# A two-layer attention and recurrence step on one core: engine queues ordered by the scheduler's finer timing model, first loads pinned in program order

## The chip, the cores and the metric

The kernel runs on 1 core of one Trainium2 chip. The metric is the device time of one launch in microseconds. The kernel before took 906.66 us (median of 3 runs, 905.13 to 910.31). In what follows PE is TensorE, ACT is ScalarE, DVE is VectorE, POOL is GpSimd and SP is SyncE; SP issues the loads that matter here.

## The reference

One inference step of a trunk of two layers over 128 context tokens and 512 latent tokens of width 1024. Each layer modulates its input by a shift and scale from SiLU(cond), mixes the tokens, gates the branch by a SiLU path, projects it out, and ends in a residual and a layer norm. Layer 0 mixes by grouped attention (16 heads, 4 key heads, rotary positions), layer 1 by HGRN2, a gated linear recurrence over 8 heads with one scan forward and one backward. Cut to what matters:

```python
for i in range(DEPTH):                       # 2 layers
    hp = xp * (1.0 + sc_p) + sh_p            # context;  hs likewise for latent tokens
    if i == 0:
        out_p, kp, vp = _attn_context(hp, ...)
        out_s = _attn_latent(hs, cache_k, cache_v, ...)
    else:
        out_p, sp_fw, sp_bw = _rec_mix(hp, zeros, zeros, ...)
        out_s, _, _ = _rec_mix(hs, state_fw, state_bw, ...)
    xp = _layer_norm(alpha * xp + g_p * out_p, ...)

def _rec_mix(h, s0_fw, s0_bw, w_in, lb, norm_gain, w_out):
    q, f_fw, f_bw, i_in, g = split(h @ w_in)             # five blocks of 1024 columns
    forget = lb + (1 - lb) * sigmoid(f); inp = (1 - lb) * sigmoid(-f)   # per direction
    # per head and direction: S_t = forget_t * S_{t-1} + inp_t v_t^T,  o_t = q_t S_t
    o = _rms_norm(o_fw + o_bw, norm_gain)
    return (o * silu(g)) @ w_out, s_fw, s_bw
```

The outputs are both token streams, the context's new keys and values, and its new states.

## The kernel before, in words

**Numbers.** Products are done in fp32r with operands split into a high and a low part: hi·hi, hi·lo and lo·hi are three matmuls. A weight piece of 128 x 1024 is loaded as fp32 by SP (`pump`, L198 to L211) into a ring of raw buffers; `split_piece` (L217) casts the high part on ACT (L221) and subtracts it on DVE or POOL (L222). `pump` is called ahead of and behind every split and issues loads in the order of a list, as far as the rings have room.

**Order of the work.** The program is written as generators that are woven by hand: `weave` puts projection steps beside the attention, and `Lane` steps a recurrence generator beside a projection generator by the estimated time of each step (the gaps D_LEV, D_KT and so on). The framework's scheduler then sets the order of each engine's queue from dependencies and a timing model, and puts in the semaphore waits. Each engine executes its queue in order; where an instruction must wait, those behind it in the same queue wait too.

**Stages, as the trace has them.** 0 to 72 us: x is transposed on PE (L443), the modulation computed (L264), x modulated (L450), keys and values projected (L469 to L471). 72 to 375: attention, scores L740 and L741, probabilities L835 and L838, transposes L850, product with the values L767; the query, gate and modulation projections (L334 to L336, L325 to L327, L264) lie beside it. 375 to 459: output projection (L1021 to L1023) and layer norm. 459 to 812: the recurrence, a head's projection overlapping the recurrence of the head before. 812 to 902.7: the last head's recurrence, then output projection, norm and stores.

**A head's projection** (`proj_gen`, L1098). Value and gate columns: 120 matmuls `vgps` (L1133 to L1135). Then three groups i = 0, 1, 2 (q and the two gates) of 48 matmuls `rps` (L1143 to L1145), called R below. Each group needs its weight piece split: cast L221 into `rhi`, a ring of two buffers, so that the cast of a later piece waits until the R that read that buffer are done; then subtraction L222 into `rlo`. Each group ends in an eviction: sigmoid `s` (L1165), for i = 1, 2 also a second sigmoid `s_…` (L1175) and a scaling (L1176) on ACT, and products on DVE.

**A head's recurrence** (`gla_gen`, L1240), called by the lane. It has seven levels of doubling block width. A level is 20 or 40 small matmuls `lv` (L1273 for levels 0 to 4, L1279 for 5 and 6), then a product on DVE that updates the keys in `A` (L1282), a copy `kc` of them on ACT (L1251, levels 0 to 3), a product on DVE that updates the queries (L1287), and a merge of the result (L1263). The next level's matmuls need both products and `kc`. Level 4 also has the diagonal `dg` (L1297). After level 6: transposes `kp` (L1313), their copy `kt` on ACT (L1315), state products `sp` (L1319), a chain of six state updates on DVE (L1322, L1325), the output products `op` (L1336 to L1339), squares and root (L1344, L192), normalization on DVE (L1348, L1350), transposes `oT` (L1355). The last head has no projection beside it; `tail_gen` gives it gate matmuls (`gateps`, L294) and the first output matmuls (`outp`, L1021 to L1023).

Of the kernel before, what the change touches and what calls it, by code (L numbers as in the profile page):

```python
# [18 lines left out]
P = 128  # L19
D = 1024  # L20
KT = D // P
TS = 4
# [115 lines left out]
def hybrid_step(ctx: ExitStack, tc: tile.TileContext, a: dict, o: dict):  # L138
    nc = tc.nc
# [54 lines left out]

    ahead = deque()
    order = deque()

    def pump():  # L198
        while order:
            start = order[0] in FIRST  # L200
            if len(ahead) >= (RAW_START if start else RAW_AHEAD):
                break
            src = order.popleft()
            if src[0] == "x":
                c = slice(src[1] * CW, (src[1] + 1) * CW)
                nc.sync.dma_start(xt[:, :TS, c], a["xs"][:, c].rearrange("(t p) d -> p t d", p=P))
                nc.sync.dma_start(xt[:, TS, c], a["xp"][:, c])
                continue
            raw = (raw0 if start else rawp).tile([P, 1024], F32, tag="raw", name="raw")
            nc.sync.dma_start(raw, piece(src))  # L210
            ahead.append((src, raw))  # L211

    def piece(src):
        name, c, i = src
        return a[name][c][:, i * 1024:(i + 1) * 1024]

    def split_piece(hi, lo, src, lo_eng=None):  # L217
        pump()
        got, raw = ahead.popleft()
        assert got == src, (got, src)  # L220
        nc.scalar.copy(hi, raw)  # L221
        (lo_eng or nc.gpsimd).tensor_tensor(lo, raw, hi.bitcast(F32), ALU.subtract)  # L222
        pump()
# [28 lines left out]
    def take(src):  # L252
        pump()
        got, raw = ahead.popleft()
        assert got == src, (got, src)
        return raw
# [123 lines left out]
    def lpool(name, bufs):  # L380
        return left.enter_context(pool(name, bufs))
# [8 lines left out]
    xt = gsp.tile([P, TT, D], F32, tag="gs", name="xt")  # L390
# [1042 lines left out]
    xp = lpool("xp", 3)  # L1433
# [102 lines left out]
```

## Time and profile before

| what | value |
|---|---|
| median of 3 runs | 906.66 us (905.13 to 910.31) |
| the profiled execution | 904.83 us |
| its span | 902.7 us |
| mean granted PE clock | 0.987 |
| PE busy | 853.8 us (95%) |
| DVE, ACT, POOL busy | 560.8, 374.2, 217.9 us |
| PE busy in 518 to 800 | 281.54 of 282.00 us |

The span runs from the first to the last instruction that the profile shows; the profiled execution's own time is 2.1 us longer. Busy time counts an instruction from its start to its modelled end, and matmuls overlap, so that the difference between two starts is the time a matmul takes up. The granted clock is given as a share of full speed. In a row of the timeline the brackets give the idle time of the engine ahead of the instruction, and the instruction that ended it.

### The profile page before, as it was taken

To read this page: it belongs to the slowest core of one execution; us is meant where nothing else is said; L and a number is where in the kernel's file an instruction comes from. 1 tells how busy PE (TensorE), PEld (TensorE's weight loads), DVE (VectorE), ACT (ScalarE), POOL (GpSimd) and SP (SyncE) were. 2 spreads that over 40 slices of the span, in tenths; PEclk is the share of its full clock that TensorE was granted. 3 is DMA by queue.
4 is the path that set the end of the run, shared out by engine and by line. 5 is a ranking of instruction groups with operands and counts; after the bars stand their busy time and mean duration, and the time that the engine had idled before them with its cause. 6 is when DMAs were issued, how large, how long until landed. Compare 5 with 4: busy or idle time off the path is not lost.

```text
span 902.7 us, 19256 instructions
## 1 busy us (share of the span) xinstructions
PE 853.8 (95%) x8116; PEld 741.6 (82%) x8116; DVE 560.8 (62%) x990; ACT 374.2 (41%) x735; POOL 217.9 (24%) x251
## 2 busy tenths in 40 slices
PE   5999999999999799899999999999999999998995
PEld 3779978777777686567889999999999999996774
DVE  3466565566576565377644667585858575859495
ACT  2142565456345544532243444444444444345200
POOL 2013033233123315340000133224241404120110
PEclk9999999999999799999999999999999999998998
DMA  9932021212030224563131322323132332223121
GB/s 318 330 106 82 24 79 41 94 49 94 24 117 25 94 71 147 185 224 144 55 95 48 95 84 78 99 75 96 53 110 71 88 90 89 84 70 137 54 94 70
DMA packets 32678, 89.86 MB, mean 100 GB/s; under 512 B 4400, under 2 KB 11568, under 8 KB 32592
## 3 DMA queue, kind: packets, MB, share of 16 engines
q1 hardware_dynamic: 21984, 71.57, 23.4%
q0 software_dynamic: 3264, 9.51, 3.9%
q10 hardware_dynamic: 7344, 7.55, 2.6%
q8 instruction: 64, 1.05, 0.5%
q14 instruction: 22, 0.18, 0.1%
HBM read 79.44 MB, written 9.18 MB: 98 GB/s over the span
## 4 chain that ended last, share of the span: by engine, by line
PE 81%; DVE 8%; ACT 3%; DMA 3%; POOL 3%; issue 2%; SPq 0%; DVEq 0%; ACTq 0%; POOLq 0%
PE rps L1143 7%; PE rps L1144 6%; PE rps L1145 6%; PE vgps L1133 5%; PE pot L767 5%; PE vgps L1134 4%; PE vgps L1135 4%; PE pt L850 4%; PE adaps L264 3%; PE outp L1021 3%; PE outp L1022 3%; PE outp L1023 3%; PE lv L1273 2%; PE sc L740 2%; PE gps L325 2%
## 5 line engine op out<-in xcount | busy, mean ns | idle before, releaser
L1143 PE MATMUL rps<-h1hi,rhi 128*128 128x320 f32 x368 | 117.2, 319 | 0.0
L1144 PE MATMUL rps<-h1lo,rhi 128*128 128x320 f32 x368 | 113.7, 309 | 0.0
L1145 PE MATMUL rps<-h1hi,rlo 128*128 128x320 f32 x368 | 113.5, 308 | 0.0
L843 POOL TENSOR_SCALAR p<-p,rc 128x640 f32<-128x640 f32 x64 | 54.0, 844 | 158.0 <-DVE rc L842 144.3
L1143 PEld LDWEIGHTS rps<-h1hi,rhi 128*128 128x128 f32 x368 | 69.1, 188 | 1.3
L1144 PEld LDWEIGHTS rps<-h1lo,rhi 128*128 128x128 f32 x368 | 69.1, 188 | 0.0
L1145 PEld LDWEIGHTS rps<-h1hi,rlo 128*128 128x128 f32 x368 | 69.1, 188 | 0.0
L838 ACT ACTIVATE p<-sc,nm 128x640 f32<-128x640 f32 x64 | 50.9, 796 | 42.2 <-DVE nm L835 35.8
L222 DVE TENSOR_TENSOR rlo<-raw,rhi 128x1024 fp32r<-128x1024 f32 x32 | 46.1, 1442 | 35.1 <-ACT rhi L221 35.1
L835 DVE TENSOR_REDUCE nm<-sc 128x1 f32<-128x640 f32 x64 | 52.2, 817 | 17.5 <-PE sc L741 17.3
L1301 POOL COPY At<-near 32x160 f32<-32x160 f32 x32 | 14.0, 438 | 197.7 <-DVE near L1263 196.7
L1251 ACT COPY kc<-A 128x640 f32<-128x640 f32 x40 | 32.1, 804 | 58.8 <-DVE A L1282 51.1
L221 ACT CAST rhi<-raw 128x1024 fp32r<-128x1024 f32 x32 | 33.6, 1049 | 54.1 <-PE rps L1144 48.0
L767 PE MATMUL pot<-pts,vv 128*64 128x256 f32 x320 | 50.1, 394 | 3.0 <-DVE gs L772 2.9
L1133 PE MATMUL vgps<-rhi,h1hi 128*128 128x256 f32 x180 | 51.3, 285 | 1.2 <-ACT h1hi L957 1.2
L850 PE MATMUL pt<-small,p 128*128 128x128 f32 x320 | 51.0, 282 | 1.0 <-POOL p L843 0.4
L745 ACT COPY pts<-pt 128x512 f32<-128x512 f32 x64 | 36.6, 586 | 36.1 <-PE pt L850 35.9
L1135 PE MATMUL vgps<-rhi,h1lo 128*128 128x256 f32 x180 | 50.4, 280 | 0.4 <-DVE h1lo L958 0.4
L1134 PE MATMUL vgps<-rlo,h1hi 128*128 128x256 f32 x180 | 50.5, 281 | 0.0
L740 PE MATMUL sc<-kk,X 128*128 128x320 f32 x128 | 43.6, 349 | 5.1 <-ACT p L838 4.4
L850 PEld LDWEIGHTS pt<-small,p 128*128 128x128 f32 x320 | 37.5, 144 | 10.0 <-issue 4.4
L1133 PE MATMUL vgps<-wspare,h1hi 128*128 128x256 f32 x140 | 41.5, 297 | 0.0
(264 smaller groups left out, 2445.8 us busy)
## 6 DMA issues: line engine op xcount, KB each, us to landing
raw<-in_ada_w SPq DMA_DIRECT2D x48, 512.0 KB, 4.4
raw<-in_rec_w_in SPq DMA_DIRECT2D x40, 512.0 KB, 3.6
raw<-in_attn_w_in SPq DMA_DIRECT2D x16, 512.0 KB, 4.1
raw<-in_attn_w_out SPq DMA_DIRECT2D x8, 512.0 KB, 4.0
raw<-in_rec_w_out SPq DMA_DIRECT2D x8, 512.0 KB, 3.4
x1d<-y SPq DMA_DIRECT2D x5, 512.0 KB, 2.9
rx<-x1d POOLq DMA_DIRECT2D x20, 128.0 KB, 3.8
x1a<-rx POOLq DMA_DIRECT2D x20, 128.0 KB, 2.3
```

The costliest lines, as they stand in the source:

```text
L740: nc.tensor.matmul(out, X[:, h, t0:t0 + P], kk[:, c, k0:k1], start=True, stop=False)
L767: nc.tensor.matmul(pot[j * HD:(j + 1) * HD, :CW], vv[:, slot, c * HD:(c + 1) * HD], moving[j], start=first, stop=last)
L835: nc.vector.tensor_reduce(nm[:, 0:1], sc[:, :, :320], AX.XY, ALU.max, negate=True)
L838: nc.scalar.activation(halves(p[:]), sc[:, :, :320], AF.Exp, bias=nm[:, 0:1], accum_out=su[:, 0:1])
L843: nc.gpsimd.tensor_scalar(p, p, rs[:, 0:1], 1.0, ALU.mult, ALU.mult)
L850: nc.tensor.transpose(pt[:, i * 256 + q * P:i * 256 + (q + 1) * P], ps[q][:, (k0 + i) * P:(k0 + i + 1) * P], ident)
L1133: nc.tensor.matmul(out, h1hi[:, k, t], hi, start=(k == 0), stop=False)
L1134: nc.tensor.matmul(out, h1hi[:, k, t], lo, start=False, stop=False)
L1135: nc.tensor.matmul(out, h1lo[:, k, t], hi, start=False, stop=(k == KT - 1))
L1143: nc.tensor.matmul(ps[:, j, :320], hi[:, k, :], h1hi[:, k, t], start=(k == 0), stop=False)
L1144: nc.tensor.matmul(ps[:, j, :320], hi[:, k, :], h1lo[:, k, t], start=False, stop=False)
L1145: nc.tensor.matmul(ps[:, j, :320], lo[:, k, :], h1hi[:, k, t], start=False, stop=(k == KT - 1))
```

## The change

Two things. The tile context is opened with `schedule_with_timeline_sim=True`, so the scheduler sets the order within each engine's queue by a finer timing model. And in `pump` the loads on SP of x and of all weight pieces except those of the recurrence (`rec…`) are wrapped in `tc.keep_in_program_order`, which keeps them in the order in which the program issues them.

```diff
@@ -194,6 +194,7 @@
     ahead = deque()
     order = deque()
+    pin, pass_on = tc.keep_in_program_order, lambda ins: ins
 
     def pump():
         while order:
@@ -203,11 +204,11 @@
             if src[0] == "x":
                 c = slice(src[1] * CW, (src[1] + 1) * CW)
-                nc.sync.dma_start(xt[:, :TS, c], a["xs"][:, c].rearrange("(t p) d -> p t d", p=P))
-                nc.sync.dma_start(xt[:, TS, c], a["xp"][:, c])
+                pin(nc.sync.dma_start(xt[:, :TS, c], a["xs"][:, c].rearrange("(t p) d -> p t d", p=P)))
+                pin(nc.sync.dma_start(xt[:, TS, c], a["xp"][:, c]))
                 continue
             raw = (raw0 if start else rawp).tile([P, 1024], F32, tag="raw", name="raw")
-            nc.sync.dma_start(raw, piece(src))
+            (pass_on if src[0][:3] == "rec" else pin)(nc.sync.dma_start(raw, piece(src)))
             ahead.append((src, raw))
@@ -1527,7 +1528,7 @@
-    with tile.TileContext(nc) as tc:
+    with tile.TileContext(nc, schedule_with_timeline_sim=True) as tc:
         hybrid_step(tc, a, o)
```

A line is added, so that line numbers from L198 on are greater by one after the change (L1143 becomes L1144). Each engine has the same instructions as before, in another order: 4359 of PE's 6310 instructions stand elsewhere (by up to 207 places), 737 of DVE's 992 (up to 17), 379 of ACT's 668 (up to 11), 32 of POOL's 256 (up to 6). SP's 144 rows stand as they did. In each of the seven heads that overlap a projection the change is the same in kind. Three places follow.

ACT in the fourth of these heads, from the copy for level 3 to the copy of the transposes and what follows it; `s` and `s_8082` are the sigmoids of the projection, `wspare` is another buffer for the cast's result. Before:

```order
L1251 COPY kc<-A 128x640
L221 CAST wspare<-raw 128x1024
L221 CAST rhi<-raw 128x1024
L1306 COPY At<-lv 32x5x32 x4
L1165 ACTIVATE s<-rps 128x640
L1306 COPY At<-lv 64x5x64 x2
L1315 COPY kt<-kp 128x1024
L221 CAST rhi<-raw 128x1024
L1165 ACTIVATE s<-rps 128x640
L1175 ACTIVATE s_8082<-rps 128x640
L1176 ACTIVATE A<-s_8082,omlb 128x640
```

And after:

```order
L1252 COPY kc<-A 128x640
L222 CAST wspare<-raw 128x1024
L222 CAST rhi<-raw 128x1024
L1166 ACTIVATE s<-rps 128x640
L1252 COPY kc<-A 128x640
L1307 COPY At<-lv 32x5x32 x4
L1307 COPY At<-lv 64x5x64 x2
L222 CAST rhi<-raw 128x1024
L1166 ACTIVATE s<-rps 128x640
L1176 ACTIVATE s_8082<-rps 128x640
L1316 COPY kt<-kp 128x1024
L1177 ACTIVATE A<-s_8082,omlb 128x640
```

The last `kc` of the head (needed by level 4) has gone behind the cast `rhi` and the sigmoid of group 0, and `kt` behind the cast and both sigmoids of group 1.

PE in the same head, at level 4. Before:

```order
L1273 MATMUL lv<-A,kc 32x32 x20
L1297 MATMUL dg<-q,kd 32x32 x20
L1143 MATMUL rps<-h1hi,rhi 128x320
L1144 MATMUL rps<-h1lo,rhi 128x320
L1145 MATMUL rps<-h1hi,rlo 128x320
```

And after, from the last R ahead of level 3 to the first behind level 5:

```order
L1144 MATMUL rps<-h1hi,rhi 128x320
L1274 MATMUL lv<-A,kc 32x32 x20
L1145 MATMUL rps<-h1lo,rhi 128x320
L1146 MATMUL rps<-h1hi,rlo 128x320
L1144 MATMUL rps<-h1hi,rhi 128x320
L1145 MATMUL rps<-h1lo,rhi 128x320
L1146 MATMUL rps<-h1hi,rlo 128x320
L1274 MATMUL lv<-A,kc 32x32 x20
L1298 MATMUL dg<-q,kd 32x32 x20
L1280 MATMUL lv<-A 32x32 x20
L1144 MATMUL rps<-h1hi,rhi 128x320
```

Before, 18 R lay between levels 3 and 4 and 18 between `dg` and level 5; after, 43 R lie ahead of level 3 (back to level 2), five between levels 3 and 4, and none between level 4 and level 5. Likewise `kp` and `sp`, with 12 R between them before, follow each other at once in these heads.

PE in the last head, from level 6 (before) and from level 3 (after). Before:

```order
L1279 MATMUL lv<-A 64x64 x10
L294 MATMUL gateps<-small,gcol_77 128x128 x4
L1021 MATMUL outp<-w_9604,ghi 128x512
L1313 MATMUL kp<-small,A 128x128 x8
L1022 MATMUL outp<-w_9605,ghi 128x512
L1023 MATMUL outp<-w_9604,glo 128x512
L1021 MATMUL outp<-w_9604,ghi 128x512
L1022 MATMUL outp<-w_9604,ghi 128x512
L1023 MATMUL outp<-w_9604,glo 128x512
L1319 MATMUL sp<-v,kt 128x128 x8
```

And after:

```order
L1274 MATMUL lv<-A,kc 32x32 x20
L295 MATMUL gateps<-small,gcol_77 128x128 x4
L1274 MATMUL lv<-A,kc 32x32 x20
L1298 MATMUL dg<-q,kd 32x32 x20
L1280 MATMUL lv<-A 32x32 x20
L1280 MATMUL lv<-A 64x64 x10
L295 MATMUL gateps<-small,gcol_77 128x128 x4
L1314 MATMUL kp<-small,A 128x128 x8
L1320 MATMUL sp<-v,kt 128x128 x8
```

Output matmuls stood between the levels; now they stand ahead of level 3 (in longer runs) and behind `oT`, and from level 3 to `oT` only the gate matmuls stand between. Between `op` and `oT` there were twelve output matmuls, and now there are four gate matmuls.

In attention, PE's order has the scores of later units further ahead of the products with the values; ACT and DVE follow. In the front a few transposes stand earlier on PE.

## The prediction

> **What bounds the kernel now.** The page of the profile comes first: its span, the busy time of the engines, and the chain that ended last.
>
> ```profile
> span 902.7 us, 19256 instructions
> PE 853.8 (95%) x8116; PEld 741.6 (82%) x8116; DVE 560.8 (62%) x990; ACT 374.2 (41%) x735; POOL 217.9 (24%) x251
> PE 81%; DVE 8%; ACT 3%; DMA 3%; POOL 3%; issue 2%; SPq 0%; DVEq 0%; ACTq 0%; POOLq 0%
> ```
>
> TensorE (PE) is busy for 95% of the span and holds 81% of the chain. Next come the windows by stage: attention (72 to 375), the eight recurrence heads with the next head's projection beside them (518 to 800), the last head (800 to 858) and the end. The columns after the window are its length, the busy time of PE, PEld, DVE, ACT and POOL, the granted clock, the DMA share and GB/s.
>
> ```profile
> 72.00:375.00 303.00, 289.40 (x2191) 233.71 (x2189) 180.57 (x366) 150.11 (x313) 89.42 (x85) 0.98 0.23 78
> 518.00:800.00 282.00, 281.54 (x3723) 272.29 (x3722) 192.03 (x294) 128.26 (x253) 85.06 (x114) 1.00 0.28 84
> 800.00:858.00 58.00, 51.53 (x574) 43.78 (x573) 36.83 (x63) 22.64 (x52) 6.29 (x9) 0.94 0.26 90
> 858.00:902.80 44.80, 34.10 (x146) 26.80 (x144) 33.57 (x60) 0.00 (x0) 5.93 (x7) 0.93 0.22 82
> ```
>
> From 518 to 800 PE idles 0.5 us in 282: whatever it waits there, the end moves. Attention has 13.6 us of idle time, the last head 6.5, the end 10.7. So a new order can win little and, in the heads, can only lose. Third is the timeline of one head around its levels 3 to 5, from PE, then ACT, then DVE (start, duration, engine, line, operation, and in brackets the idle time before it with its releaser):
>
> ```profile
> 642.27 0.56 PE L1273 MATMUL lv<-A,kc 128*32 128x32 f32 x40
> 645.59 0.53 PE L1273 MATMUL lv<-A,kc 128*32 128x32 f32 x38
> 645.97 0.54 PE L1297 MATMUL dg<-q,kd 128*32 128x32 f32 x38
> 646.44 0.42 PE L1143 MATMUL rps<-h1hi,rhi 128*128 128x320 f32 x1
> 649.04 0.31 PE L1145 MATMUL rps<-h1hi,rlo 128*128 128x320 f32 x1
> 649.28 0.53 PE L1279 MATMUL lv<-A 128*32 128x32 f32 x37
> ...
> 643.78 0.73 ACT L1251 COPY kc<-A 128x640 f32<-128x640 f32 x1 [2.72 <-DVE A L1282]
> 649.24 1.05 ACT L221 CAST rhi<-raw 128x1024 fp32r<-128x1024 f32 x1 [3.31 <-PE rps L1144]
> ...
> 642.87 0.83 DVE L1282 TENSOR_TENSOR A<-A,Tb 128x640 f32<-128x640 f32 x1 [0.58 <-PE lv L1273]
> 644.54 0.83 DVE L1287 TENSOR_TENSOR A<-A,Tb 128x640 f32<-128x640 f32 x1 [0.60 <-ACT kc L1251]
> ```
>
> From level 3 (642.27) the chain is PE, DVE L1282, ACT kc, DVE L1287, then level 4 (645.59). PE never waits, because projection matmuls (rps, called R here) lie between: 18 R from 646.44 to 649.28, 0.158 us each. The weight cast L221 waits for an R matmul (3.31 us, without harm), because the ring has two buffers. Hence two things keep PE fed: enough R between two levels, and kc ahead of that cast on ACT's in-order queue.
>
> **The change, part by part.** Every engine gets the instructions it had; no term is an added or removed one. The pins leave all 144 rows of SP as they were: 0, with nothing to hide, since nothing is queued behind another load than before. What moves is PE, ACT and DVE. The durations needed are in the groups by form, from 518 to 800 (busy us, mean ns of one):
>
> ```profile
> L222 DVE TENSOR_TENSOR rlo<-raw,rhi 128x1024 fp32r<-128x1024 f32 x24 | 36.4, 1515 | 23.4 <-ACT rhi L221 23.4
> L221 ACT CAST rhi<-raw 128x1024 fp32r<-128x1024 f32 x24 | 25.2, 1049 | 37.7 <-PE rps L1144 35.8 <-PE vgps L1135 1.9
> L1251 ACT COPY kc<-A 128x640 f32<-128x640 f32 x30 | 24.1, 804 | 44.7 <-DVE A L1282 37.7 <-DVE A L1177 7.0
> L1165 ACT ACTIVATE s<-rps 128x640 f32<-128x640 f32 x18 | 12.6, 700 | 0.1
> L1175 ACT ACTIVATE s<-rps 128x640 f32<-128x640 f32 x12 | 8.3, 695 | 0.0
> L1315 ACT COPY kt<-kp 128x1024 f32<-128x1024 f32 x6 | 6.1, 1015 | 22.4 <-PE kp L1313 22.4
> ```
>
> Level 4. In the new order 43 R come ahead of level 3, five behind it, and then level 4, the diagonal dg and level 5 with nothing between. On ACT the cast rhi and the sigmoid s stand ahead of kc. The cast waits for the 47th R of the group, s for the 48th; kc, and DVE L1287 behind it, come after. From the end of the 47th R: 1.05 (cast) + 0.70 (s) + 0.80 (kc) + 0.83 (L1287) = 3.4, and some 0.05 at each of four hand-offs, 3.6. The subtraction L222, now ahead of L1287 on DVE, takes 1.5 beside s and kc, which take 1.5 too. PE has one R left, so it waits about 3.5 us. Behind this wait stand all of PE's later work and, through it, everyone's.
>
> Level 5. DVE does L1282 and L1287 again (1.66); PE has level 4 and dg meanwhile (645.59 to 646.44, 0.85). Wait 0.8. Before, 18 R filled it.
>
> sp. In the second group the order on ACT is cast, s, s_8082, kt, and on PE kp is followed by sp at once. From the 47th R: 1.05 + 0.70 + 0.70 + 1.02 = 3.5. PE has one R (0.15) and kp (0.9 to 1.0, the row of kp below). Wait 2.4; with hand-offs 2.5. Before, 12 R hid it.
>
> A head loses 3.5 + 0.8 + 2.5 = 6.8 us; seven heads overlap a projection: 47.6. It can be less only if PE had R left to run, and the queue is in order.
>
> The clock. Two waits of before were followed by a halved clock: 4.09 us in attention and 3.45 us in the last head.
>
> ```profile
> 306.31 0.64 PE L740 MATMUL sc<-kk,X 128*128 128x320 f32 x1 [4.09 <-ACT p L838]
> 816.89 0.76 PE L1273 MATMUL lv<-A,kc 128*32 128x32 f32 x40 [3.45 <-ACT kc L1251]
> ...
> 305.66:315.90 10.24, 9.59 (x44) 7.64 (x45) 2.77 (x8) 4.23 (x10) 2.64 (x3) 0.50 0.21 74
> 811.00:814.25 3.25, 0.96 (x7) 0.53 (x5) 3.19 (x4) 3.02 (x5) 1.48 (x3) 1.00 0.63 233
> 814.25:821.08 6.83, 4.19 (x52) 3.83 (x53) 6.09 (x7) 5.41 (x8) 0.00 (x0) 0.50 0.76 273
> ```
>
> At clock 0.50 half of the busy time is lost: 4.8 us of 9.59 in the first, 2.1 of 4.19 in the second. The second drop began when PE had still worked 0.96 of 3.25 us, so little work does not prevent it. A wait of 3.5 us, a burst of 0.85 and one of 0.8 make such a stretch in every head, and by the phase of that window I expect it to be caught in 6 of 7 heads, at 2.2 us (nearer to the second row, since waits behind it swallow part): 13 us. Bounds: 0, and 7 × 4.8 = 34. The Trainium skill's page "TensorE: Matmul & The Clock Gate", in "What's actually happening", says that the clock halves after at least one idle window of about 3.4 us on a free-running grid; read as a wholly idle window, a wait of 3.5 us would seldom contain one, and the 13 us would be near 0. The row 811.00 to 814.25, with 0.96 us of work ahead of the drop, disagrees with that strict reading, so I keep the 13.
>
> The last head. In before, output matmuls stand between its levels; in the new order none stands from level 3 to oT, and those taken out run later without hiding anything.
>
> ```profile
> 830.67 0.56 PE L1273 MATMUL lv<-A,kc 128*32 128x32 f32 x40
> 834.09 0.53 PE L1273 MATMUL lv<-A,kc 128*32 128x32 f32 x38
> 835.97 0.55 PE L1279 MATMUL lv<-A 128*32 128x32 f32 x40
> 838.51 0.80 PE L1279 MATMUL lv<-A 128*64 128x64 f32 x20
> 840.48 1.03 PE L1313 MATMUL kp<-small,A 128*128 128x128 f32 x8
> 842.62 2.05 PE L1319 MATMUL sp<-v,kt 128*128 128x128 f32 x16
> 854.67 0.74 PE L1355 MATMUL oT<-small,on 128*128 128x128 f32 x5 [1.33 <-DVE on L1350]
> ...
> 846.01 0.34 DVE L1325 SCALAR_TENSOR_TENSOR S<-S,Tb,sp 128x128 f32<-128x128 f32 x1
> ```
>
> Level 3 to level 4: chain 0.56 + 0.83 + 0.80 + 0.83 = 3.0 against 1.0 of PE's own (level and four small gate matmuls), wait 2.0 (the gate matmuls at half of the eight of kp). To level 5: 0.8. To level 6: two DVE products against one level, 1.6. To kp 0.3. To sp: 842.62 less 840.48 less 1.03, 1.1. To the first op: the state chain ends at 846.35, sp at 844.67, 1.7. From op to oT about 4.5: the eviction chain of squares, root and products lay there beside twelve matmuls, and PE still waited 1.33. Sum 12.0, less the 1.33 that is there already, 10.7. At the head's start oT and the first kc now stand behind weight casts, as estimate well under 1 us more. I take 11; bounds 6 (if the smaller waits overlap) and 16.
>
> The front and the attention. The front's order differs little: +2 (bounds 0 and 6, as its idle time is small against the load's). In attention the scores are set further ahead: the stall of 4.09 may shrink, and with it 4.8 of half clock. At best all idle time and that loss go: −13.6 − 4.8 = −18. At worst the idle time doubles and three more stalls bring half clock: 13.6 + 3 × 4.8 = +28. I take −4, about half of the one stall and of its half clock, as PE's order there keeps its pattern.
>
> Sum: 47.6 + 13 + 11 + 2 − 4 = 69.6. On the profiled execution's 904.83 us that is 974.4. The median of the runs, 906.66, lies 1.8 above it: 976.
>
> **The rivals.** First, the waits come, but the clock stays full: no 13, so 963. For it: the wait of level 4 is only as long as the 3.45 us that was caught once, and the R ahead of it and level 4 and dg behind it (0.85 us) put work on both sides. Against: the row with 0.96 us of work ahead of the drop. The strict reading of the Trainium skill's page, above, ends here too.
>
> Second, faster: attention gains its 18 us and the heads lose less than that, 2.6 us each. It decides at ACT's queue: only if kc and kt come before the casts there, or the cast finds its ring buffer free earlier, are the head's waits short. The order speaks against it in each of the seven heads; the row of the cast (3.31 us waiting for PE L1144) says that the buffer is not free. At waits of 0.5 us a head (3.5) and the last head at 6 it would be 906.7 + 3.5 + 6 − 18 = 898.
>
> Third, no change: the order only renames what PE does anyway, as it is 95% busy. That gives 907. It holds if R still lies ahead of each waiting instruction; the order puts kp and sp side by side.
>
> Fourth, slower still: attention's banks are reused sooner and it loses up to 28 instead of winning 4: 976 + 32 = 1008, or about 1000 with most of it.
>
> **How the numbers follow.** The forecast has 0.52; waits at full clock 0.32; slower still 0.08; faster 0.05; no change 0.03. Of these, all but the last two are slower by over 0.5%, which is about what a measurement of this kernel can tell from no change: 0.92. The range takes the full-clock case with attention's gain at its bound (963 − 14 = 949) and above the forecast half of the clock's spread up to its bound of 34 and some of the attention's (976 + 11 + 11 = 998). That leaves out the faster and unchanged cases (0.08) and much of the fourth (0.06), and some for terms I mis-size: 948 to 998.
>
> **What would show it.** Right: in the changed profile the windows of the heads grow by some 60 us; ahead of level 4 (L1274) stands an idle time near 3.5 us, released by DVE A L1288 or ACT kc L1252; ahead of sp (L1320) some 2.5 us, released by ACT kt; the cast and s run between. PE's clock shows about six windows of 0.50 in the heads; the last head takes 10 us longer. Wrong: kc running ahead of the cast; waits below 1 us ahead of level 4; a clock of 1.00 through the heads (then 963); or a change of more than 15 us in attention.

## The result, and the profile after

The changed kernel takes 999.11 us (median of 4 runs, 997.6 to 1001.56), the kernel before 907.97 us beside it (median of 4 runs, 905.13 to 910.31). The ratio is 1.1008, with a 95% interval of 1.0966 to 1.105. The forecast was 976 with a range to 998: the sign and the place were right, the size was 23 us short. The profiled execution took 1001.56 us. From its page, the span, the busy time of the engines and the chain that ended last:

```profile
span 999.5 us, 19228 instructions
PE 893.7 (89%) x8116; PEld 776.1 (78%) x8116; DVE 558.0 (56%) x990; ACT 372.7 (37%) x735; POOL 209.8 (21%) x251
...
PE 80%; DVE 9%; ACT 5%; DMA 2%; issue 2%; POOL 0%; SPq 0%; DVEq 0%; ACTq 0%; POOLq 0%
```

PE's share of the span fell from 95% to 89%, but its busy time rose by 40 us, with as many instructions. Both are losses: PE waits more, and what it does takes longer. The windows by stage show where. First the kernel before, cut at the same events (attention from the first score matmul to the last product with the values; heads from the first R to the last; last head up to its `oT`; the end):

```profile
108.40:379.20 270.80, 257.66 (x1955) 201.61 (x1954) 157.45 (x326) 138.17 (x296) 85.36 (x84) 0.98 0.25 84
462.60:810.90 348.30, 347.82 (x4472) 337.03 (x4472) 227.35 (x351) 156.63 (x305) 90.28 (x124) 1.00 0.29 85
810.90:855.10 44.20, 37.73 (x478) 30.74 (x477) 31.61 (x51) 17.48 (x35) 5.03 (x8) 0.92 0.28 100
855.10:902.70 47.60, 37.01 (x159) 28.94 (x157) 34.46 (x61) 0.80 (x1) 5.93 (x7) 0.93 0.21 78
```

And the kernel after:

```profile
109.30:392.40 283.10, 268.26 (x1956) 207.45 (x1954) 159.77 (x330) 138.65 (x297) 82.25 (x84) 0.95 0.25 81
476.50:892.90 416.40, 373.16 (x4474) 360.87 (x4472) 222.54 (x350) 154.75 (x305) 84.35 (x123) 0.93 0.25 71
892.90:949.30 56.40, 39.52 (x478) 33.28 (x477) 32.06 (x51) 17.61 (x35) 5.54 (x9) 0.90 0.23 78
949.30:999.50 50.20, 38.00 (x159) 30.03 (x157) 34.33 (x61) 0.79 (x1) 6.01 (x7) 0.91 0.20 74
```

The heads grew by 68.1 us, attention by 12.3, the last head by 12.2, the end by 2.6, front and output projection together by 1.6. Each stage's time is taken apart as follows: idle is the length less PE's busy time; the loss to half clock is half of PE's busy time in the stretches with a granted clock of 0.50; what is left is the work at full clock. A stretch that lies across the bound of two stages is counted in both.

| stage | idle before, after | half-clock stretches before, after | lost to half clock before, after | work left before, after |
|---|---|---|---|---|
| attention | 13.1, 14.8 | 1, 5 | 4.8, 14.6 | 252.9, 253.7 |
| seven heads | 0.5, 43.2 | 0, 12 | 0.0, 28.0 | 347.8, 345.2 |
| last head | 6.5, 16.9 | 1, 3 | 2.1, 4.3 | 35.7, 35.3 |
| end | 10.6, 12.2 | 1, 2 | 0.0, 1.3 | 37.0, 36.7 |

The work left is the same within 3 us in every stage, so waits and half clock account for the loss: some 56 us of waits and 41 of half clock. The list of what PE waited for, after the change (total, times, longest; the last head is in these totals):

```profile
PE lv L1274 <- DVE A L1288: 23.6, 8, 3.2
PE sp L1320 <- ACT kt L1316: 17.5, 8, 2.3
PE lv L1280 <- DVE A L1288: 7.7, 9, 2.0
PE sc L741 <- ACT p L839: 7.2, 7, 2.3
PE adaps L265 <- DMA raw<-in_ada_w: 7.0, 5, 3.1
...
PE oT L1356 <- DVE on L1351: 4.1, 1, 4.1
```

None of the first three was in the list of before with more than 0.3 us in the heads. The timeline of one head shows them; PE first, then ACT, then DVE:

```profile
633.47 0.56 PE L1274 MATMUL lv<-A,kc 128*32 128x32 f32 x40
634.50 0.31 PE L1145 MATMUL rps<-h1lo,rhi 128*128 128x320 f32 x1
634.65 0.31 PE L1146 MATMUL rps<-h1hi,rlo 128*128 128x320 f32 x1
638.11 0.76 PE L1274 MATMUL lv<-A,kc 128*32 128x32 f32 x40 [3.15 <-DVE A L1288]
639.82 0.76 PE L1280 MATMUL lv<-A 128*32 128x32 f32 x40 [0.40 <-DVE A L1288]
653.87 2.34 PE L1320 MATMUL sp<-v,kt 128*128 128x128 f32 x14 [2.34 <-ACT kt L1316]
...
634.85 1.05 ACT L222 CAST rhi<-raw 128x1024 fp32r<-128x1024 f32 x1 [2.48 <-PE rps L1145]
635.80 0.70 ACT L1166 ACTIVATE s<-rps 128x640 f32<-128x640 f32 x1
636.40 0.71 ACT L1252 COPY kc<-A 128x640 f32<-128x640 f32 x1
650.54 1.05 ACT L222 CAST rhi<-raw 128x1024 fp32r<-128x1024 f32 x1 [2.70 <-PE rps L1145]
652.79 1.02 ACT L1316 COPY kt<-kp 128x1024 f32<-128x1024 f32 x1
...
635.93 1.23 DVE L223 TENSOR_TENSOR rlo<-raw,rhi 128x1024 fp32r<-128x1024 f32 x1 [0.79 <-ACT rhi L222]
637.14 0.82 DVE L1288 TENSOR_TENSOR A<-A,Tb 128x640 f32<-128x640 f32 x1
```

This is the chain of the prediction. The cast starts at 634.85, 0.04 us after the 47th R (634.50, and 0.31 long) has ended; the sigmoid and `kc` follow; on DVE the subtraction, then L1288; then level 4 at 638.11. The subtraction and `kc` end together (637.16 and 637.11). For sp the chain runs on ACT alone: the cast at 650.54, both sigmoids, `kt` from 652.79 to 653.81, then sp at 653.87. The clock of this head, in the stretches ahead of its two drops and in the drops themselves:

```profile
634.53:637.94 3.41, 0.43 (x3) 0.17 (x2) 2.62 (x4) 2.26 (x3) 0.00 (x0) 1.00 0.53 159
637.94:644.77 6.83, 6.25 (x136) 6.08 (x137) 4.94 (x11) 1.13 (x4) 3.70 (x6) 0.50 0.27 80
651.60:655.01 3.41, 1.14 (x10) 1.15 (x11) 2.57 (x3) 2.93 (x4) 0.00 (x0) 1.00 0.35 90
655.01:658.42 3.41, 3.41 (x17) 3.41 (x16) 1.64 (x6) 0.02 (x1) 0.00 (x0) 0.50 0.20 80
```

There are two drops in the head, one behind level 4's wait and one behind sp's. PE is busy in nearly all of their time: they cost (6.25 + 3.41) / 2 = 4.8 us in this head. Level 4's wait is followed by a drop in all seven heads, sp's in five of them: twelve in all.

### The profile page after: what moved, and what is told of

Same layout as the page of the kernel before. It is cut to its first block, busy times and chain, and to the rows that moved or that the text cites. A ratio compares the mean times of both kernels' runs of the same rounds, so it can differ in the third digit from the quotient of the medians.

```text
span 999.5 us, 19228 instructions
## 1 busy us (share of the span) xinstructions
PE 893.7 (89%) x8116; PEld 776.1 (78%) x8116; DVE 558.0 (56%) x990; ACT 372.7 (37%) x735; POOL 209.8 (21%) x251
## 4 chain that ended last, share of the span: by engine, by line
PE 80%; DVE 9%; ACT 5%; DMA 2%; issue 2%; POOL 0%; SPq 0%; DVEq 0%; ACTq 0%; POOLq 0%
PE rps L1144 7%; PE rps L1145 6%; PE rps L1146 6%; PE pot L768 5%; PE vgps L1134 4%; PE vgps L1135 4%; PE vgps L1136 4%; PE pt L851 4%; PE outp L1022 3%; PE outp L1023 3%; PE outp L1024 3%; PE adaps L265 2%; PE sc L741 2%; PE sp L1320 2%; DMA raw<-in_ada_w 2%; PE gps L326 2%
## 5 line engine op out<-in xcount | busy, mean ns | idle before, releaser
L1144 PE MATMUL rps<-h1hi,rhi 128*128 128x320 f32 x368 | 124.5, 338 | 0.2 <-issue 0.2
L1145 PE MATMUL rps<-h1lo,rhi 128*128 128x320 f32 x368 | 121.8, 331 | 0.0
L1146 PE MATMUL rps<-h1hi,rlo 128*128 128x320 f32 x368 | 119.9, 326 | 0.0
L1144 PEld LDWEIGHTS rps<-h1hi,rhi 128*128 128x128 f32 x368 | 76.2, 207 | 1.8 <-issue 0.6
L1145 PEld LDWEIGHTS rps<-h1lo,rhi 128*128 128x128 f32 x368 | 75.9, 206 | 0.3
L1146 PEld LDWEIGHTS rps<-h1hi,rlo 128*128 128x128 f32 x368 | 75.4, 205 | 0.0
L1302 POOL COPY At<-near 32x160 f32<-32x160 f32 x32 | 18.2, 568 | 235.6 <-DVE near L1264 234.6
L223 DVE TENSOR_TENSOR rlo<-raw,rhi 128x1024 fp32r<-128x1024 f32 x32 | 42.4, 1325 | 31.0 <-ACT rhi L222 31.0
L768 PE MATMUL pot<-pts,vv 128*64 128x256 f32 x320 | 55.8, 406 | 0.2 <-DVE gs L773 0.2
L1283 DVE TENSOR_TENSOR A<-A,T 128x640 f32<-128x640 f32 x32 | 26.4, 824 | 41.8 <-PE lv L1280 30.3
L851 PEld LDWEIGHTS pt<-small,p 128*128 128x128 f32 x320 | 38.9, 149 | 12.2 <-issue 9.4
```

Of the source, the lines that this page charges most:

```text
L768: nc.tensor.matmul(pot[j * HD:(j + 1) * HD, :CW], vv[:, slot, c * HD:(c + 1) * HD], moving[j], start=first, stop=last)
L851: nc.tensor.transpose(pt[:, i * 256 + q * P:i * 256 + (q + 1) * P], ps[q][:, (k0 + i) * P:(k0 + i + 1) * P], ident)
L1144: nc.tensor.matmul(ps[:, j, :320], hi[:, k, :], h1hi[:, k, t], start=(k == 0), stop=False)
L1145: nc.tensor.matmul(ps[:, j, :320], hi[:, k, :], h1lo[:, k, t], start=False, stop=False)
L1146: nc.tensor.matmul(ps[:, j, :320], lo[:, k, :], h1hi[:, k, t], start=False, stop=(k == KT - 1))
```

## The experiments

Theory: in each of the seven heads the new queues make PE wait (43 us), and each wait is followed by half clock that costs time of its own (28 us); the last head loses 12, attention the rest. Rivals: that the half clock hides in the waits or has another origin; that one queue alone (ACT's, or PE's) makes the waits; that the pins cost the time. To change one queue and leave the others as they are, most kernels fix each engine's queue instruction by instruction, by an issue-order edge from each to the one ahead of it; the lists are those of the two kernels' own queues, and can be cut and joined at the stages' bounds:

```diff
     with tile.TileContext(nc, schedule_with_timeline_sim=True) as tc:
         hybrid_step(tc, a, o)
+        impose(tc, QUEUES)      # per engine: the order of its instructions
+
+def impose(tc, queues):
+    for eng, text in queues.items():
+        mine = [i for i in traced if i.engine == getattr(mybir.EngineType, eng)]
+        for at in ...:          # each behind the one ahead of it in the list
+            tc.add_manual_dep(mine[at], last, mybir.DependencyInfo(mybir.DependencyClass.NoSync, ...))
```

**The heads alone, in both directions.** The queues of the seven heads are exchanged: those of before in the changed kernel, and those of after in the kernel before.

```diff
-QUEUES = after
+QUEUES = after[front, attention, out] + before[seven heads] + after[last head, end]    # heads_of_before
+QUEUES = before[front, attention, out] + after[seven heads] + before[last head, end]   # heads_of_after
```

> The changed program, but in the seven heads that overlap a projection the queues of PE, ACT and DVE stand in the order of before; front, attention, output projection and last head stand as after the change. Theory (waits made by the order in the heads, 43 us, and half clock that follows them, 28 us): both go, 999 - 71 = 928, range 922 to 935, and no window of half clock is left in the heads. Rival (the half clock in the heads is not caused by the waits there, it lasts from the attention on): only the 43 go, 956.

> The mirror image: everything in the order of before, only the seven heads in the order after the change. Theory: 907 + 71 = 978, range 971 to 985, with twelve or so windows of half clock in the heads. Rival (half clock comes from elsewhere): 907 + 43 = 950.

Measured: 929.31 us (926.35 to 932.64) and 974.76 us (972.28 to 977.98). The windows of attention, heads and last head with the heads of before, and then attention and heads with the heads of after:

```profile
108.60:391.70 283.10, 268.32 (x1956) 207.49 (x1955) 159.83 (x330) 138.68 (x297) 82.28 (x84) 0.95 0.24 81
475.80:824.00 348.20, 347.61 (x4473) 336.81 (x4472) 227.43 (x351) 156.63 (x305) 90.27 (x124) 1.00 0.28 85
824.00:880.50 56.50, 39.62 (x478) 33.34 (x477) 32.21 (x51) 17.59 (x35) 5.04 (x8) 0.90 0.22 78
```

```profile
110.00:381.80 271.80, 258.52 (x1954) 202.90 (x1954) 157.42 (x326) 138.24 (x296) 85.37 (x84) 0.97 0.25 84
465.10:880.80 415.70, 372.40 (x4473) 360.36 (x4472) 222.43 (x350) 154.86 (x305) 84.44 (x123) 0.93 0.24 72
```

The heads take 348.2 us with the one order and 415.7 with the other, whatever stands around them; attention's 12 us and the last head's 12 stay with their own queues. The stages add up, and the half clock of the heads goes and comes with the order of the heads.

**The clock alone.** In the changed order, matmuls whose results are overwritten are put ahead of level 4 and sp, into the banks that these write next. PE's wait is then filled with work.

```diff
             pt = wide(bank2("lv"))
+            if lev == 4 and h < RH - 1:
+                fill(pt, 22)
...
         sp = bank2("sp")
+        if h < RH - 1:
+            fill(wide(sp), 17)
+# fill: n times nc.tensor.matmul(out[:, :320], h1hi[:, 0, :P], h1hi[:, 0, :320], start=True, stop=True)
```

> The changed order to the instruction, with 22 matmuls whose results are overwritten put ahead of level 4 and 17 ahead of sp in each of the seven heads, in the banks that level 4 and sp write next; PE has work during the two waits, and the waits themselves stay. Theory (the half clock follows from PE's idling and costs time of its own): the twelve half-clock windows of the heads go, 28 us less: 971, range 965 to 980. Rival (the half clock hides in the waits, or is not set by PE's activity): 999, or up to 10 more where the filling work outlasts a wait.

Measured: 979.2 us (977.38 to 981.29). The window of the heads:

```profile
473.10:866.60 393.50, 387.50 (x4747) 376.96 (x4745) 225.34 (x350) 154.92 (x305) 84.84 (x123) 1.00 0.26 76
```

The granted clock is 1.00 throughout, and the heads take 393.5 us instead of 416.4, with 273 matmuls more. So the half clock in the heads follows from PE's idling and costs time of its own: without it the heads are 23 us shorter. Of the 28 expected, 5 are not seen: filling and remaining idle time come to 48 us where 43 had been idle (393.5 less the 345.2 of work), so the filling outlasts the waits by about that much.

A second run put in only six such matmuls ahead of level 4 and none ahead of sp.

> The changed order with six instead of 22 filling matmuls ahead of level 4 (0.9 us of work) and none ahead of sp. In the traces so far every stretch of 3.41 us on the clock's grid with less than 1.4 us of PE work was followed by half clock, none with more than 2.4 us. Theory: the stretches of level 4 get from 0.4 to 1.1 up to 1.3 to 2.0 us of work, so about half of their drops go, those at sp stay: 10 of the 28 us less, 989, range 982 to 996. Rival 1 (only a wholly idle stretch halves the clock): the drops of level 4 all go, 978. Rival 2 (any wait over 3 us does it, whatever the work): 999.

Measured: 992.33 us (987.12 to 996.17), with six half-clock stretches in the heads instead of twelve. The size is the expected one, but which drops went is not. Five of level 4's seven drops stayed, with 1.1 to 1.4 us of work in the stretch ahead of each; sp is followed by one drop instead of five, although nothing was put ahead of it and its wait is still 2.34 us in every head. Three stretches of this run, ahead of a drop at level 4, ahead of a drop at sp, and at an sp that had none:

```profile
629.33:632.74 3.41, 1.10 (x82) 0.81 (x80) 3.10 (x5) 1.46 (x3) 0.00 (x0) 1.00 0.48 151
701.01:704.42 3.41, 1.07 (x9) 0.97 (x9) 2.58 (x3) 3.09 (x5) 0.00 (x0) 1.00 0.26 48
537.17:540.58 3.41, 1.61 (x14) 1.61 (x15) 2.13 (x3) 2.48 (x4) 0.00 (x0) 1.00 0.46 136
```

The same wait of sp leaves 1.07 to 1.77 us of work in its stretch, as it falls on the clock's grid, and only at 1.07 was the clock halved. The first rival (only a wholly idle stretch halves the clock) falls with the five drops that stayed. The second is not tested cleanly, since the filling also cut level 4's wait from 3.15 to 2.19 us.

**Which queue makes the waits.** Three edits to the changed order, in the seven heads, PE's queue untouched. The first moves `kc` and `kt` on ACT; the second also moves a product on DVE; the third puts DVE's subtraction further back.

```diff
 ACT:  kc(3)  wspare-cast
+      kc(4)
       rhi-cast  s
-      kc(4)
       At  At
+      kt
       rhi-cast  s  s_8082
-      kt                                       # act_only: these lines
 DVE:  L1264
+      L1288(3)                                 # ahead_of_casts: and these
       L223 rlo
-      L1288(3)
       L1283(4)  L1287  L1288(4)  merges
+      L223 rlo                                 # sub_behind: rlo here instead
```

> The changed order with only ACT's queue edited in the seven heads: kc of level 4 ahead of the cast rhi, kt ahead of the next cast; DVE's subtraction of that cast still stands ahead of L1287 of level 3. Theory (two queues hold level 4, ACT's and DVE's, and DVE's subtraction needs the same cast): level 4 still waits about 3.1 us, released by DVE; level 5 0.7; sp 1.1 instead of 2.3: 7 x 1.2 = 9 less, and a few us of half clock behind sp: 987, range 979 to 994. Rival (the wait of level 4 is ACT's queue): level 4 falls to 1.7 too, 975 or less.

> The changed order, with three kinds of instruction moved in each of the seven heads: on ACT the copy kc of level 4 ahead of the cast rhi, and kt ahead of the next cast; on DVE L1287 of level 3 ahead of the subtraction. PE's queue stays. Theory (casts ahead and too few R between are both needed for the whole wait): level 4 waits 1.9 us instead of 3.15, sp 1.1 instead of 2.3, level 5 as it is; 7 x 2.4 = 17 less, and about half of the 28 us of half clock: 968, range 960 to 984. Rival 1 (the casts' place alone makes the waits): the heads are as before, 928. Rival 2 (PE's own order alone): 999.

> As with both queues edited, but the subtraction on DVE goes behind all of level 4's products and merges instead of directly behind L1287 of level 3. Theory (there the wait was handed on to level 5, which waited 2.1 us instead of 0.7): level 4 waits 1.7, level 5 0.8, sp 1.1: the heads idle 25 us instead of 35, and half clock falls from 20 to about 10 us: 982 - 9 - 9 = 964, range 956 to 974. Rival (the wait is handed on again, to level 6 or to the next group's R, whose low part comes later): 982.

Measured: 988.99 us (987.93 to 989.25), 981.58 us (980.27 to 986.72) and 972.1 us (968.68 to 973.67). What PE waited for in the three, in this order (L1293 is levels 0 to 4, L1299 levels 5 and 6, L1339 sp; each total includes the last head):

```profile
PE lv L1293 <- DVE A L1307: 28.8, 8, 4.3
PE sp L1339 <- ACT kt L1335: 8.8, 8, 1.1
...
PE lv L1299 <- DVE A L1307: 6.6, 9, 2.0
```

```profile
PE lv L1299 <- DVE A L1307: 18.1, 9, 2.3
PE lv L1293 <- DVE A L1307: 13.6, 8, 2.1
PE sp L1339 <- ACT kt L1335: 8.8, 8, 1.1
```

```profile
PE lv L1293 <- DVE A L1307: 13.6, 8, 2.1
PE lv L1299 <- DVE A L1307: 9.5, 9, 1.9
PE sp L1339 <- ACT kt L1335: 8.8, 8, 1.1
```

With ACT's queue alone mended, sp's wait halves (17.5 to 8.8) and level 4's does not fall: DVE's subtraction holds it. It even rises, from 3.15 to 3.83 us in six of the heads, where 3.1 was expected: `kc` now runs ahead of the cast, so that the cast and the subtraction come later. With DVE's product moved too, level 4's wait falls from 23.6 to 13.6, but level 5's rises from 7.7 to 18.1: the subtraction now stands ahead of its products. That was not in the expectation, which had 968 us, though the time still lies in its range. With the subtraction behind both, level 5's returns to 9.5. The wait thus goes along DVE's queue to whoever stands behind the subtraction. What stays in the third (1.66, 0.9 and 1.10 us in a head) is PE's own order: five R, none and none where the chains take 3.0 us and less. Both rivals with one cause fall: of the 68 us that the heads had lost, the third edit takes back 31.5 (its heads take 384.9 us), and the rest is put down to PE's order, which the next run changes. The mirror image, PE's order of before with ACT's order after the change, was not tried: there `kc` stands behind a cast that waits for an R, and that R behind level 4, which needs `kc`, so that the two queues would wait for each other.

**What mends it within the scheduler.** Flag and pins as in the change, and only PE held in program order from the first head to the end of the last.

```diff
+    with in_order(tc, mybir.EngineType.PE):      # each PE instruction behind the one traced ahead of it
     for h in range(RH):
         ...
+    with in_order(tc, mybir.EngineType.PE):
     weave((1.0 for _ in lane.gens[0][0]), side, SIDE_T)
```

> Flag and pins as in the change, and PE's queue held in program order from the first head to the end of the last one; ACT and DVE are ordered by the scheduler, which then puts kc and kt ahead of the casts by itself. Theory: the heads come back to about 353 us (12 R between levels 3 and 4 leave 0.7 us of wait in each head), the last head is about 12 us shorter than after the change, front and attention keep their loss: 999 - 66 - 12 = 921, range 912 to 930, no half clock in the heads. Rival (ACT's and DVE's queues under this scheduler make the waits by themselves): heads stay above 390, 960 or more.

Measured: 934.16 us (932.94 to 934.63). The windows of heads and last head:

```profile
473.20:831.00 357.80, 348.83 (x4474) 337.22 (x4472) 225.33 (x351) 155.77 (x305) 83.30 (x124) 1.00 0.28 83
831.00:879.70 48.70, 35.94 (x466) 29.33 (x466) 31.61 (x51) 17.47 (x35) 3.98 (x8) 0.91 0.26 90
```

The heads come back to 357.8 us with a clock of 1.00, and the rival falls. The time lies 4 us above the range: the heads gain 58.6 us where the sum had 66, and the last head 7.7 instead of 12. ACT's and DVE's queues follow PE's: with R between the levels, the scheduler itself puts `kc` and `kt` ahead of the casts.

**Flag without pins.**

```diff
-    pin, pass_on = tc.keep_in_program_order, lambda ins: ins
+    pin = pass_on = lambda ins: ins
```

> The finer timing model without the pins: the scheduler then moves loads of the first weights on SP (key and value pieces behind query pieces), and the heads' queues are those of the change. Theory (the loss is the flag's, the pins only keep the first loads in place): heads 416 us as after the change, and the front some us later: 1003, range 998 to 1012. Rival (the pins cost the attention its time): about 10 less, 989.

Measured: 997.22 us (996.91 to 1000.22). The heads take 415.7 us again. Neither expectation was met: the front is as long (109.2 us) though the loads stand otherwise; attention is 10 us shorter (273.0), with two half-clock stretches instead of five, and the output projection 6 us longer, with two stretches of its own. The sum is that of the change: the pins move time between stages, but change nothing in the total that can be told.

**A version that might beat both.** The order of before, with after's order where before has its 4.09 us stall in attention, and 24 filling matmuls in the last head's first wait.

```diff
-QUEUES = before
+QUEUES = before, but PE 1698:1794, DVE 339:354, ACT 203:219, POOL 65:67 from after
...
+            if lev == 0 and h == RH - 1:
+                fill(pt, 24)
```

> The order of before with two edits: between 287 and 307 us (about PE's 1700th to 1800th instruction) PE, ACT, DVE and POOL run in the order after the change, which had no 4.1 us stall there; and 24 filling matmuls stand ahead of the last head's first level, in its wait of 3.45 us. Theory: the first edit saves 3 us (0 to 8, as half clock may still follow), the second the 2.1 us of half clock: 906 - 5 = 901, range 896 to 906. Rival (half clock moves to other stretches, waits come back later): no change, 906.

Measured: 910.18 us (905.98 to 912.83, 12 runs); ratio 1.0033, 1.0013 to 1.0053. It is not faster, but 0.3% slower. The two places, in its timeline (PE, and then ACT in the last head):

```profile
309.09 0.41 PE L768 MATMUL sc<-kk,X 128*128 128x320 f32 x1 [3.98 <-ACT p L866]
...
817.71 3.77 PE L1295 MATMUL lv<-h1hi 128*128 128x320 f32 x24
823.52 0.63 PE L1307 MATMUL lv<-A,kc 128*32 128x32 f32 x40 [2.05 <-ACT kc L1279]
...
821.51 1.04 ACT L249 CAST w<-raw 128x1024 fp32r<-128x1024 f32 x1 [2.01 <-PE lv L1295]
822.46 1.01 ACT L1279 COPY kc<-A 128x640 f32<-128x640 f32 x1
```

The stall came back behind the exchanged stretch (3.98 us). In the last head the half clock did go, but level 0 still waited 2.05 us behind the filling, where 3.45 us had been the whole wait: on ACT a cast that stands ahead of `kc` started only when the filling had ended (821.48), whereas in the kernel before the same cast waited for nothing (814.89). The filling delayed what it should only bridge; why the cast waits for it was not looked into. No version faster than before was found.

## Why the prediction was off, step by step

**Level 4, level 5, sp.** Taken as 3.5, 0.8 and 2.5 us a head; measured 3.15, 0.4 to 1.0 and 2.34. The sum of 47.6 us stands against 42.7 of additional idle time. The order of the queues, the durations from before and the waits of a two-buffer ring were enough to say this. One detail came out only in the experiments: the subtraction on DVE, which the prediction names as running beside `s` and `kc`, is a second lock of the same size. That does not change the sum. Nor does it that the prediction takes 518 to 800 us for the eight heads: its rows hold six (six copies `kt`), and the sum goes by the seven that overlap a projection.

**The clock.** This is the step that failed: "I expect it to be caught in 6 of 7 heads, at 2.2 us", 13 us in all. Measured are 12 stretches in seven heads and 28.0 us, plus 9.8 us more than before in attention, 2.2 in the last head and 1.3 at the end: 41 us. Three things were mis-sized. sp's wait was given no drop, since only waits of 3.45 us and more had been seen to bring one; at 2.34 us it is caught in five heads, for 8.5 us. Level 4's is caught in all seven heads, and at 2.8 us each instead of 2.2 (19.4 us): the price was taken from the second row of before, where PE was idle for 2.6 of 6.83 us of half clock, but behind the heads' waits PE has R to do and is busy in 91% of the half-clock time. And attention was thought to gain. The bound of 34 us that stood for the heads held; the range went only half of the way to it. The strict reading of the Trainium skill's page "TensorE: Matmul & The Clock Gate" (the section "What's actually happening"), by which only a wholly idle window counts, fails in this case: none of the twelve drops here follows a stretch without work (0.35 to 1.46 us of it in each).

**Attention.** Taken as −4 with bounds of −18 and +28; it lost 12.3. Idle time rose by only 1.7 us; the stall of 4.09 us went, as expected, but the new ones are many (7.2 us for the scores over seven waits, a load that came 3.1 us late) and five stretches of half clock follow. With the same queues in attention, the stage took 277.6 to 283.1 us in the runs above, and its half-clock loss 7.3 to 14.6 us: one of its drops after the change follows a stretch with 2.3 us of work, so that small shifts may decide. Neither that nor which of its many moves brings which drop was tried.

**The last head, front, output projection.** 11 expected, 12.2 measured, of which 10.4 are waits; front and output projection 2 and 1.6. The longest new wait is the predicted one from `op` to `oT` (4.1 us). The end, for which nothing was set down, lost 2.6.

**The miss as a sum.** On the profiled execution 974.4 us was forecast and 1001.56 measured, 27 more. The heads' half clock makes 15 of it (28.0 for 13), attention 16 (12.3 for −4), the end and the last head 4; the heads' waits and work came out 7.5 lower. So the clock's term and attention's failed by about the same amount, and most of attention's loss is half clock too.

**The rivals.** Full clock (963) is refuted by the clock in the traces and by the filled run. Faster and unchanged are refuted. The one "slower still", near 1000, was right in size, and its reason (attention) in part: its chance of 0.08 was too small, since half clock makes most of both attention's loss and the miss in the heads.

## What to carry to other kernels

When a change only reorders queues, find for each in-order queue the instruction that waits on PE (here a cast into a two-buffer ring), and see what was put behind it; if PE's next step needs that, the chain can be added up from durations of the old profile, and mending one queue can hand the wait to the next. Price the clock separately: count the stretches of 3.4 us that would hold little PE work, and take half of the work in the one or two stretches behind each as lost. A finer model of time in the scheduler did not give a better order here: 43 R ahead of level 3 spent early the independent matmuls that had covered the chains.

## What the runs showed of the hardware

In the twelve profiles of this case (the two kernels and the ten others) the halved clock starts and ends on a grid of 3.413 us. Counting PE's work in each full-clock stretch of that grid, between the first score and the end of the last head (each matmul from its start to its end or to the next one's start): of 98 stretches with less than 1.25 us of work, all were followed by half clock; of 165 with 1.25 to 2.5 us, 32 were; of some 2340 with more than 2.5 us, none. So in these runs it is the work in a stretch, and not whether a whole one is idle, that goes with the clock: with less than about a third of it busy the clock was always lost, with more than about three quarters never, and in between these counts do not decide. A wait of 2.34 us (sp) could be enough, by where it lay on the grid: it was in five heads of the changed kernel, and in one where level 4's wait had been filled in part.
